# Down projection of a two-layer trunk: twelve instead of eight of 22 row tiles by seven products, the ordinary row tiles as lead

## The chip, the cores and the metric

The kernel runs on one core of a Trainium2 chip. A core has five engines that work side by side, each with an instruction queue of its own: TensorE (PE, matmuls and transposes), VectorE (DVE), ScalarE (ACT), GpSimd (POOL, here it issues accumulating DMAs) and SyncE (SP, here it issues loads and stores). SBUF is the working memory, PSUM holds matmul results in eight banks. The metric is device time in microseconds of one execution, the median of several runs.

## The reference

Two layers. Each layer is a half-step SwiGLU, a mixer (a gated linear recurrence and a windowed attention), and a second half-step SwiGLU, each with an RMS norm before and after it:

```python
def swiglu(h, w_gate, w_up, w_down):
    return (jax.nn.silu(h @ w_gate) * (h @ w_up)) @ w_down
...
for l in range(DEPTH):
    h = rms_norm(x, gn[0])
    x = x + 0.5 * rms_norm(swiglu(h, w_ffn1_gate[l], w_ffn1_up[l], w_ffn1_down[l]), gn[1])
    ...  # mixer
    h = rms_norm(x, gn[4])
    x = x + 0.5 * rms_norm(swiglu(h, w_ffn2_gate[l], w_ffn2_up[l], w_ffn2_down[l]), gn[5])
```

There are 512 tokens, 1024 model columns and 2816 inner columns, all in float32. The part in question is the product with `w_down`: (512 x 2816) @ (2816 x 1024), four times in the program. The 2816 inner columns are 22 row tiles of 128.

## The kernel before

**Float32 by three matmuls.** Every operand is split into a high part rounded to the fast format (`hi`, float32r) and the low rest (`lo`). A product is hi x hi + hi x lo + lo x hi, three matmuls (`mm3`). ScalarE makes the high part with a copy, VectorE the low part with a subtraction; `split_dma` makes the low part in another way, by a second ScalarE pass (the negated value) and an accumulating DMA that POOL issues.

**Weights.** `Stream` brings the weights in the order in which TensorE uses them. A raw unit of 128 x 1024 is loaded into `w32` (four buffers) by SP and rounded into `whi` and `wlo` (six buffers each, `WS`). An item is one rounded unit. Up to three items are made ahead (`AHEAD`), as long as fewer than six are in use. `Stream.quarter` makes the items of the seven products.

**The order of the work.** The order of TensorE's instructions is that of the program text; short side jobs (the recurrence, the attention, transposes) are put between by an estimate of the time (`Order`, `WAIT`). The instructions of the other engines are ordered at build time by a scheduler that works with its own estimates, except where `pin` keeps program order. On the chip each queue is then fixed. SBUF tiles of 128 x 512 come from one pool of 61 buffers (`big`), PSUM banks from two pools: five `acc` and three `aux`.

**The down projection (`down`, L636).** Its result is 512 x 1024: four token tiles `t` and two column halves `h`, eight accumulators `y[t][h]` of one bank each. `both(j, h)` adds two row tiles (2j and 2j+1) to one half: 4 x 2 x 3 = 24 matmuls of 128 x 512, with one weight item. Here the rows of the left operand, `src`, are split by `ready` shortly before they are used.

Eight of the 22 row tiles go by a scheme with seven instead of eight block products. The left operand is cut into two halves of tokens and two groups of row tiles, the weights into two groups of row tiles and two halves of columns; sums of these blocks are multiplied (products 1 to 7), and the results are added up. One product with four row tiles and two token tiles is 4 x 2 x 3 = 24 matmuls. `Late.sums` makes the sums of the left operand (`quarter_sums`: four VectorE operations of 128 x 256 per pair of row tiles) and splits them; `quarters` runs the products and adds the results with VectorE; products 2, 3 and 4 go straight into `y`.

So there is first a lead (row tiles 0 to 7, half 0, four calls of `both`), in which the operands of the products are made; then the products 1, 6, 2, 7, 5, 4, 3; then the last six row tiles of half 0; then the 14 ordinary row tiles of half 1. During the last four units of half 1 the results leave PSUM: `half` adds the products' sums and multiplies by the gains, `post` and `norm` add to x and normalize, `turn` transposes for the next stage. The rows of x and the gains come by `fetch`, ahead of half 1.

**The mixer.** `recurrence_scores` computes score blocks in steps. Between the steps it yields, and other matmuls run. The step after `WAIT["chunks"]` (1270 in the estimate's nanoseconds) is four matmuls of 128 x 256 on operands that VectorE scales at L1047 and L1048, with a copy by ScalarE at L1057.

Of the kernel before, what the change touches and what calls it, by code (L numbers as in the profile page):

```python
# [15 lines left out]
P = 128  # L16
D = 1024
S = 512
# [15 lines left out]
    head=2600.0, level=5000.0, last=3400.0, chunks=1270.0, blocks=350.0, norm=2370.0, gate=8000.0,  # L34
# [4 lines left out]
LEAD = 8  # L39
ORDER = ("p1", "p6", "p2", "p7", "p5", "p4", "p3")  # L40
DMAS = ()
# [4 lines left out]
def trunk(ctx: ExitStack, tc: tile.TileContext, xin, wall, gains, lbT, hgain, sinks, c_dist, c_mask, c_ident, out):  # L46
# [109 lines left out]
    class Stream:  # L156
# [36 lines left out]
        def rows(self, kt, fast):  # L193

            u0 = self.wall

            def pieces(j, h):
                b = [(4 * h + i) * kt + 2 * j for i in range(4)]  # L200
                return [(slice(i * 2 * P, (i + 1) * 2 * P), wall[u0 + n // 8][:, n % 8 * P : (n % 8 + 2) * P]) for i, n in enumerate(b)]

            def unit(j, h):
                c = 2 * j * P
                self.src[self.n] = [(None, wall[u0 + 4 * h : u0 + 4 * h + 4, :, c : c + 2 * P].rearrange("u p c -> p u c"))] if kt == 8 else pieces(j, h)
                self.plain(1)

            j0, later = LEAD // 2 if fast else 0, []
            if fast:
                for j in range(j0):  # L210
                    unit(j, 0)

                u = self.n
                for q in range(2):
                    self.src[u + q] = pieces(j0 + q, 0)
                    self.src[u + 2 + q] = pieces(j0 + 2 + q, 0)
                self.side[u + 1] = [pieces(j0 + q, 1) for q in range(4)]
                for k in ORDER:
                    for q in range(2):
                        it = Item(k, u + q + (2 if k in ("p2", "p4") else 0), 4)  # L220
                        it.base, it.q = u, q
                        self.items.append(it)
                self.t2 = [None, None]
                self.n += 4
                for j in range(j0):
                    later.append(j)
                j0 += 4
            for j in range(j0, kt // 2):
                unit(j, 0)
                later.append(j)  # L230
            for j in later:
                unit(j, 1)
            self.wall = u0 + kt

        def load(self, upto):
            while self.dma < min(upto, self.n):
                w = sb.tile([P, D], F32, tag="w32", name=nm("w32"), bufs=W32)
                u = self.dma
                if isinstance(self.src[u], list):
                    for c, a in self.src[u]:  # L240
                        nc.sync.dma_start(w.rearrange("p (m c) -> p m c", m=4) if c is None else w[:, c], a)
                else:
                    for c in (slice(0, D // 2), slice(D // 2, D)) if u == 0 else (slice(0, D),):
                        nc.sync.dma_start(w[:, c], wall[self.src[u]][:, c])
                self.raw[u] = w
                self.dma += 1
                if u in self.side:
                    self.b12, self.b22 = [], []
                    for i, ps in enumerate(self.side[u]):
                        v = [big(), big()]  # L250
                        for c, a in ps:
                            nc.sync.dma_start(v[c.start // S][:, c.start % S : c.start % S + 2 * P], a)
                        (self.b22 if i > 1 else self.b12).append(v)

        def quarter(self, it):

            self.load(it.base + 4)
            q, h = it.q, (slice(0, S), slice(S, D))
            if it.kind in ("p1", "p2", "p5", "p4"):
                w = [self.raw[it.u][:, c] for c in h]  # L260
            elif it.kind == "p6":

                t = sb.tile([P, D], F32, tag="tt", name=nm("tt"), bufs=2)
                self.t2[q] = w = [t[:, c] for c in h]
                for c in range(2):
                    t1 = self.raw[it.u][:, h[c]]
                    pin(nc.vector.tensor_tensor(t1, t1, self.b12[q][c], op=ALU.subtract))
                    pin(nc.vector.tensor_tensor(w[c], t1, self.b22[q][c], op=ALU.subtract))  # L268
            elif it.kind == "p3":
                w = self.b22[q]  # L270
            elif it.kind == "p7":

                w = self.b12[q]
                for c in range(2):
                    b21 = self.raw[it.base + 2 + q][:, h[c]]
                    pin(nc.vector.tensor_tensor(w[c], w[c], self.b22[q][c], op=ALU.add))
                    pin(nc.vector.tensor_tensor(b21, b21, self.t2[q][c], op=ALU.add))
            it.hi = sb.tile([P, D], F32R, tag="whi", name=nm("whi"), bufs=WS)
            it.lo = sb.tile([P, D], F32R, tag="wlo", name=nm("wlo"), bufs=WS)
            for c in range(2):  # L280
                nc.scalar.copy(it.hi[:, h[c]], w[c])
                if it.kind in DMAS:
                    nc.scalar.mul(it.lo[:, h[c]], w[c], -1.0)
                    nc.gpsimd.dma_start(it.lo[:, h[c]].bitcast(F32), w[c], accum_op=ALU.add)
                else:
                    nc.vector.tensor_tensor(it.lo[:, h[c]], w[c], it.hi[:, h[c]].bitcast(F32), op=ALU.subtract)  # L286
            self.done += 1
            self.flight += 1
            if it.kind in ("p5", "p4"):
# [181 lines left out]
    class Quarters:  # L471
# [4 lines left out]
        def operand(self, n):  # L476
# [4 lines left out]
            return [[v[:, i, :] for v in x[k]] for k in range(4)]  # L481
# [127 lines left out]
    class Late(Quarters):  # L609


        def __init__(self, src, k0):
            self.src, self.k0 = src, k0
            self.x1, self.x56, self.x37, self.t = [], [], [], []


        def sums(self):
            k = self.k0 + len(self.x56)
            a = [self.src[i][:, c] for i in (k, k + 4) for c in HALF]
# [3 lines left out]
            self.x56.append(pair_split(s))  # L623
            self.t.append(t)
            self.src[k] = ()

        def more(self, n):

            for i in range(len(self.x37), n):
                self.src[self.k0 + 4 + i] = split(self.src[self.k0 + 4 + i])  # L630
                self.x37.append(pair_split(self.t[i], split_dma))

        def raw(self, half, i):
            return [cut(self.src[self.k0 + 4 + k], HALF[half]) for k in range(4)] if i else self.x1

    def down(src, kt, l, n, nxt, fast):  # L636
# [8 lines left out]
        pre = Pre(*nxt) if nxt else None  # L645

        def ready(n):

            for i in range(min(n, kt)):
# [6 lines left out]
        def piece(b, t, h, j, i):  # L656
            st = cut(src[2 * j + i], slice(t * P, (t + 1) * P))
            mm3(y[t][h], st, [halves(w, i) for w in b[2:]], 2 * j + i == 0 and not (fast and h and t < 2), 2 * j + i == kt - 1)
# [20 lines left out]
        js = list(range(kt // 2))  # L679
        if fast:  # L680
            late = Late(src, LEAD)
            for j in range(LEAD // 2):
                ready(2 * j + EARLY)
                while len(late.x56) < min(4, 8 * (j + 1) / LEAD):
                    late.sums()
                both(j, 0)
            more = quarters(late, y)
            del js[LEAD // 2 : LEAD // 2 + 4]
        for j in js[LEAD // 2 if fast else 0 :]:
            ready(2 * j + 2 + EARLY)  # L690
            both(j, 0)
        if not fast:
            for t in range(TT):
                y[t][1] = aux() if t > 1 else acc()
        fetch()
        last = js[-TAIL:]
        for j in js[:-TAIL]:
            both(j, 1)

        warm = small([P, 1], "warm", 2)  # L700
        pin(nc.scalar.activation(out=warm, in_=src[last[0]][0][:, :1].bitcast(F32), func=AF.Sqrt, bias=eps_t, scale=0.0))
# [69 lines left out]
    def quarters(late, y):  # L771
# [3 lines left out]
        def product(n, o, start, stop=True):  # L775
            its = [ws.whole(), ws.whole()]
            for k in range(4):
                for t in range(2):
                    st = cut(late.operand(n)[k], slice(t * P, (t + 1) * P))
                    it = its[k // 2]  # L780
                    mv = [w.rearrange("p (m two c) -> p m two c", two=2, c=P)[:, :, k % 2, :] for w in (it.hi, it.lo)]
                    mm3(o[t], st, mv, start and k == 0, stop and k == 3)
# [12 lines left out]
        late.more(2)  # L795
        p = product(1, two(acc), True)
        p1, u2, u3, c12, c22 = (two(big) for _ in range(5))
        for t in range(2):
            nc.scalar.copy(p1[t], p[t])
        late.more(4)  # L800

        add(u2, product(6, two(aux), True), p1)
        product(2, [y[t][0] for t in (0, 1)], False, False)

        add(u3, product(7, two(acc), True), u2)
        p = product(5, two(aux), True)
        add(c12, p, u2)
        add(c22, p, u3)
        product(4, [y[t][0] for t in (2, 3)], False, False)
        for t in range(TT):  # L810
            y[t][1] = aux() if t > 1 else acc()
        product(3, [y[t][1] for t in (0, 1)], True, False)
# [638 lines left out]
```

## Time and profile before

| | |
|---|---|
| median of 3 runs | 2108.14 us (2106.92 to 2108.67) |
| the profiled execution's own time | 2106.95 us |
| its span, first to last instruction | 2104.9 us |
| TensorE busy | 2093.2 us |
| VectorE busy | 1549.3 us |
| ScalarE busy | 1122.6 us |
| granted TensorE clock, mean | 0.999 |
| the four down projections begin at | 241.1, 937.4, 1282.6, 1978.6 us |

In a group's line `L115 PE MATMUL acc<-whi,s 128*128 128x512 f32 x1264 | 414.0, 393 | 0.0` the first number behind the bar is the busy time of the group in microseconds, the second the mean of one in nanoseconds, the last the idle time of the engine just before them, with what ended it. Matmuls overlap each other, so their mean duration is longer than the distance between two. In the windows, each row is a stretch: its length, then busy time and count of PE, the weight loads, DVE, ACT and POOL, the granted clock, the DMA engines' busy share, and GB/s. `w<-wall` and `s<-wall` are loads of weights, `s<-s` at L400 and L401 the two halves of a split (cast and subtraction), L281 and L286 those of the seven products' weights, L324 and L331 those of the others. L458 to L462 are the sums in `quarter_sums`.

### The profile page before, as it was taken

To read this page: it belongs to the slowest core of one execution; us is meant where nothing else is said; L and a number is where in the kernel's file an instruction comes from. 1 tells how busy PE (TensorE), PEld (TensorE's weight loads), DVE (VectorE), ACT (ScalarE), POOL (GpSimd) and SP (SyncE) were. 2 spreads that over 40 slices of the span, in tenths; PEclk is the share of its full clock that TensorE was granted. 3 is DMA by queue.
4 is the path that set the end of the run, shared out by engine and by line. 5 is a ranking of instruction groups with operands and counts; after the bars stand their busy time and mean duration, and the time that the engine had idled before them with its cause. 6 is when DMAs were issued, how large, how long until landed. Compare 5 with 4: busy or idle time off the path is not lost.

```text
span 2104.9 us, 35214 instructions
## 1 busy us (share of the span) xinstructions
PE 2093.2 (99%) x13549; PEld 1875.4 (89%) x13549; DVE 1549.3 (74%) x2705; ACT 1122.6 (53%) x1899; POOL 154.2 (7%) x188
## 2 busy tenths in 40 slices
PE   9999999999999999999999999999999999999998
PEld 7899988877888999998899998898778989999987
DVE  5877886766776777789587778767686758777884
ACT  6555554446454555556355556444654545555562
POOL 0011000000000011110001110000000000111000
PEclk9999999999999999999999999999999999999999
DMA  8677653312236357774447775632122563677651
GB/s 247 152 181 184 176 164 127 111 61 70 72 101 201 127 123 181 181 194 128 151 114 176 183 181 149 190 121 91 51 81 61 136 190 106 158 182 181 182 164 47
DMA packets 148071, 298.35 MB, mean 142 GB/s; under 512 B 16992, under 2 KB 74816, under 8 KB 147904
## 3 DMA queue, kind: packets, MB, share of 16 engines
q1 hardware_dynamic: 122416, 228.16, 33.1%
q0 software_dynamic: 25344, 67.91, 18.7%
q8 instruction: 106, 1.74, 0.3%
q14 instruction: 61, 0.50, 0.1%
q10 hardware_dynamic: 144, 0.05, 0.0%
HBM read 213.43 MB, written 14.73 MB: 108 GB/s over the span
## 4 chain that ended last, share of the span: by engine, by line
PE 80%; DVE 9%; ACT 6%; issue 2%; DMA 2%; SPq 0%; ACTq 0%; DVEq 0%
PE acc L115 59%; PE aux L115 19%; ACT whi L324 2%; DMA w<-wall 2%; DVE s L401 1%; PE aux L125 1%; DVE wlo L331 1%; DVE wlo L286 1%; ACT s L400 1%; ACT m L894 1%; ACT wlo L328 1%; PE acc L125 1%; DVE tt L318 1%; DVE tt L311 1%; DVE tt L268 0%
## 5 line engine op out<-in xcount | busy, mean ns | idle before, releaser
L115 PE MATMUL acc<-s,whi 128*128 128x256 f32 (+1 forms) x4952 | 1059.4, 311 | 0.9 <-ACT whi L324 0.7
L115 PEld LDWEIGHTS acc<-s,whi 128*128 128x128 f32 x4952 | 808.0, 191 | 51.8 <-issue 3.2
L115 PE MATMUL acc<-s,wlo 128*128 128x256 f32 (+1 forms) x2476 | 766.6, 310 | 0.1
L115 PEld LDWEIGHTS acc<-s,wlo 128*128 128x128 f32 x2476 | 472.6, 191 | 25.2 <-DVE wlo L331 0.4
L324 ACT CAST whi<-w 128x1024 fp32r<-128x1024 f32 (+1 forms) x341 | 317.0, 948 | 259.2 <-PE acc L115 99.9
L115 PE MATMUL acc<-whi,s 128*128 128x512 f32 x1264 | 414.0, 393 | 0.0
L324 ACT CAST whi<-tt 128x1024 fp32r<-128x1024 f32 x154 | 161.4, 1048 | 326.6 <-DVE tt L318 182.8
L331 DVE TENSOR_TENSOR wlo<-w,whi 128x1024 fp32r<-128x1024 f32 (+1 forms) x181 | 218.1, 1215 | 156.5 <-ACT whi L324 149.4
L115 PEld LDWEIGHTS acc<-whi,s 128*128 128x128 f32 x1264 | 237.1, 188 | 54.9 <-ACT whi L324 1.6
L331 DVE TENSOR_TENSOR wlo<-tt,whi 128x1024 fp32r<-128x1024 f32 x154 | 188.0, 1221 | 97.4 <-ACT whi L324 97.3
L115 PE MATMUL acc<-wlo,s 128*128 128x512 f32 x632 | 246.9, 391 | 1.0 <-DVE wlo L286 1.0
L115 PE MATMUL aux<-s,whi 128*128 128x256 f32 (+1 forms) x1248 | 230.5, 285 | 0.0
L329 POOL DMA_DIRECT2D wlo<-w x160 | 137.8, 863 | 1259.6 <-ACT wlo L328 732.2
L115 PE MATMUL aux<-whi,s 128*128 128x512 f32 x592 | 196.8, 390 | 0.0
L115 PEld LDWEIGHTS aux<-s,whi 128*128 128x128 f32 x1248 | 195.2, 192 | 1.1 <-issue 0.5
L115 PE MATMUL aux<-s,wlo 128*128 128x256 f32 (+1 forms) x624 | 177.6, 285 | 0.0
L115 PEld LDWEIGHTS acc<-wlo,s 128*128 128x128 f32 x632 | 118.7, 188 | 25.6 <-DVE wlo L286 2.4
L115 PEld LDWEIGHTS aux<-whi,s 128*128 128x128 f32 x592 | 111.1, 188 | 22.9
L328 ACT ACTIVATE wlo<-w 128x1024 fp32r<-128x1024 f32 (+1 forms) x160 | 129.8, 844 | 0.0
L400 ACT CAST s<-s 128x512 fp32r<-128x512 f32 (+1 forms) x164 | 88.6, 580 | 70.7 <-DVE s L459 66.6
L115 PEld LDWEIGHTS aux<-s,wlo 128*128 128x128 f32 x624 | 119.8, 192 | 0.4
L115 PE MATMUL aux<-wlo,s 128*128 128x512 f32 x296 | 115.2, 389 | 0.0
(186 smaller groups left out, 2127.6 us busy)
## 6 DMA issues: line engine op xcount, KB each, us to landing
w<-wall SPq DMA_DIRECT2D x267, 512.0 KB, 3.7
wlo<-w POOLq DMA_DIRECT2D x83, 512.0 KB, 5.5
w<-wall SPq DMA_DIRECT2D x288, 128.0 KB, 3.2
wlo<-w POOLq DMA_DIRECT2D x77, 256.0 KB, 3.3
x_d<-s SPq DMA_DIRECT2D x48, 256.0 KB, 2.1
s<-x_d SPq DMA_DIRECT2D x48, 256.0 KB, 5.3
w<-wall SPq DMA_DIRECT2D x34, 256.0 KB, 3.0
s<-wall SPq DMA_DIRECT2D x64, 128.0 KB, 3.6
```

The costliest lines, as they stand in the source:

```text
L115: nc.tensor.matmul(o, lhsT, rhs, start=start, stop=stop)
L125: nc.tensor.transpose(o, src, ident)
L286: nc.vector.tensor_tensor(it.lo[:, h[c]], w[c], it.hi[:, h[c]].bitcast(F32), op=ALU.subtract)
L311: pin(nc.vector.tensor_tensor(self.t13[:, h[0]], w[:, h[0]], v[:, h[0]], op=ALU.add))
L318: pin(nc.vector.tensor_tensor(t[:, h[1]], t[:, h[0]], w[:, h[1]], op=ALU.add))
L324: i = nc.scalar.copy(it.hi[:, c], w[:, c])
L328: nc.scalar.mul(it.lo[:, c], w[:, c], -1.0)
L329: nc.gpsimd.dma_start(it.lo[:, c].bitcast(F32), w[:, c], accum_op=ALU.add)
L331: nc.vector.tensor_tensor(it.lo[:, c], w[:, c], it.hi[:, c].bitcast(F32), op=ALU.subtract)
L400: nc.scalar.copy(hi, src)
L401: nc.vector.tensor_tensor(lo, src, hi.bitcast(F32), op=ALU.subtract)
L894: nc.scalar.activation(out=m[:, 0:2, :], in_=m[:, 0:2, :], func=AF.Silu)
```

## The change

**Twelve row tiles.** `LEAD = 8` gives way to `SEVEN = 12`: row tiles 0 to 11 go by the seven products, with six row tiles each (36 matmuls), and three weight items instead of two. The ten last ones (12 to 21) are ordinary, and half 0 of all ten is the lead (five calls of `both`). Half 1 of the ten follows the products: one unit, and then the last four, in which the results leave.

**Order of the products.** 1, 3, 7, 2, 6, 4, 5. The raw side blocks (b22, b12) are six of two 128 x 512 buffers, formerly four. Sums of weights are made product by product: b12 + b22 for product 7, the block t2 from it, b22 + t2 after product 6, b21 + t2 for product 4. t2 has a buffer from `tt` or, the third, `m`. The subtraction for `wlo` is pinned to program order.

**Rounding product by product.** `late.sums` now splits a[0] (product 1) and the sums t (products 3 and 7, the low part by DMA); the sums s (products 5 and 6) and the second group of row tiles (products 2 and 4) are split only behind product 7, by `more` and `rest`, all with the low part by DMA. In the lead, a split row tile is dropped after its unit (`part`) and split again for half 1, apart from those that are already kept.

**PSUM.** `y[0][1]` and `y[1][1]` are `aux` and come behind product 1, `y[2][1]` and `y[3][1]` are `acc`, behind product 5. `fetch` now stands ahead of product 5. In the mixer, `chunks` is 2600.

```diff
-    head=2600.0, level=5000.0, last=3400.0, chunks=1270.0, blocks=350.0, norm=2370.0, gate=8000.0,
+    head=2600.0, level=5000.0, last=3400.0, chunks=2600.0, blocks=350.0, norm=2370.0, gate=8000.0,
...
-LEAD = 8
-ORDER = ("p1", "p6", "p2", "p7", "p5", "p4", "p3")
-DMAS = ()
+SEVEN = 12
+ORDER = ("p1", "p3", "p7", "p2", "p6", "p4", "p5")
...
+            lead = range(SEVEN // 2 if fast else 0, kt // 2)
+            for j in lead:
+                unit(j, 0)
             if fast:
...
+                u, n = self.n, SEVEN // 4
+                for q in range(n):
+                    self.src[u + q] = pieces(q, 0)
+                    self.src[u + n + q] = pieces(n + q, 0)
+                self.side[u + n - 1] = [pieces(n + q, 1) for q in range(n)], [pieces(q, 1) for q in range(n)]
...
-            for j in later:
+            for j in lead:
                 unit(j, 1)
...
         def quarter(self, it):
...
+            n, q, h = SEVEN // 4, it.q, (slice(0, S), slice(S, D))
+            self.load(it.base + n if it.kind == "p3" else it.u + 1)
+
+            def sums(o, x, y, op):
                 for c in range(2):
...
+                    pin(nc.vector.tensor_tensor(o[c], x[c], y[c], op=op))
+
+            raw = [self.raw[it.u][:, c] for c in h] if it.kind in ("p1", "p7", "p2", "p4") else None
+            if it.kind in ("p1", "p2"):
+                w = raw
+            elif it.kind in ("p3", "p5"):
                 w = self.b22[q]
             elif it.kind == "p7":
                 w = self.b12[q]
...
+                sums(w, w, self.b22[q], ALU.add)
+            elif it.kind == "p6":
+                w = self.t2[q]
+            else:
+                w = raw
+                sums(w, w, self.t2[q], ALU.add)
...
+                pin(nc.vector.tensor_tensor(it.lo[:, h[c]], w[c], it.hi[:, h[c]].bitcast(F32), op=ALU.subtract))
+            if it.kind == "p7":
+
+                t = sb.tile([P, D], F32, tag="m" if q == 2 else "tt", name=nm("t2"), bufs=1 if q == 2 else 2)
+                self.t2.append([t[:, c] for c in h])
+                sums(self.t2[q], raw, w, ALU.subtract)
+            elif it.kind == "p6":
+                sums(self.b22[q], self.b22[q], w, ALU.add)
...
     class Late(Quarters):
...
         def sums(self):
-            k = self.k0 + len(self.x56)
-            a = [self.src[i][:, c] for i in (k, k + 4) for c in HALF]
+            k = len(self.x1)
+            a = [self.src[i][:, c] for i in (k, k + self.n) for c in HALF]
             x = big(F32R, [P, 2, S // 2])
             self.x1.append(split(a[0], to=(x[:, 0, :], x[:, 1, :])))
             s, t = quarter_sums(a[0], a[2], a[1], a[3], True)
-            self.x56.append(pair_split(s))
-            self.t.append(t)
+            self.s.append(s)
+            self.x37.append(pair_split(t, split_dma))
             self.src[k] = ()
...
+        def rest(self):
+            for k in range(self.n, 2 * self.n):
+                self.src[k] = split_dma(self.src[k])
+
+        def more(self):
+            self.x37 = None
+            while self.s:
+                self.x56.append(pair_split(self.s.pop(0), split_dma))
...
         if fast:
...
+            late = Late(src)
+            for i, j in enumerate(js):
+                while len(late.x1) < min(late.n, (late.n * (i + 1) + 3) // 4):
                     late.sums()
+                for k in range(2 * j, min(2 * j + EARLY, kt)):
+                    if k not in part and not isinstance(src[k], tuple):
+                        part[k] = split(src[k])
                 both(j, 0)
...
+                for k in (2 * j, 2 * j + 1):
+                    part.pop(k, None)
+            more = quarters(late, y, fetch)
...
         p = product(1, two(acc), True)
+        late.x1 = None
+        p1, u3, c12, c22 = (two(big) for _ in range(4))
         for t in range(2):
             nc.scalar.copy(p1[t], p[t])
...
+        for t in range(2):
+            y[t][1] = aux()
+        product(3, [y[t][1] for t in (0, 1)], True, False)
+        p = product(7, two(acc), True)
+        late.rest()
+        late.more()
+        add(u3, p, p1)
+        product(2, [y[t][0] for t in (0, 1)], False)
+        p = product(6, two(acc), True)
+        add(c12, p, p1)
+        add(u3, p, u3)
+        product(4, [y[t][0] for t in (2, 3)], False)
+        fetch()
+        p = product(5, two(acc), True)
         add(c22, p, u3)
...
+        add(c12, p, c12)
...
-                for i in range(EARLY):
+                for i in range(SEVEN, SEVEN + EARLY):
                     a[i] = split(a[i])
```

More of the change, by code (lines that the diff above doesn't have):

```diff
@@ L769, in down, with quarters @@
         return pre
-    def quarters(late, y):
+    def quarters(late, y, fetch):
         def product(n, o, start, stop=True):
-            its = [ws.whole(), ws.whole()]
-            for k in range(4):
+            x = late.operand(n)
+            for k in range(late.n):
+                if k % 2 == 0:
+                    it = ws.whole()
+                mv = [w.rearrange("p (m two c) -> p m two c", two=2, c=P)[:, :, k % 2, :] for w in (it.hi, it.lo)]
                 for t in range(2):
[L779 to L782, printed above, removed]
+                    mm3(o[t], cut(x[k], slice(t * P, (t + 1) * P)), mv, start and k == 0, stop and k == late.n - 1)
                     ws.used((it, 1))
@@ L793, in two @@
             return [f(), f()]
-        late.more(2)
         p = product(1, two(acc), True)
-        p1, u2, u3, c12, c22 = (two(big) for _ in range(5))
+        late.x1 = None
+        p1, u3, c12, c22 = (two(big) for _ in range(4))
         for t in range(2):
             nc.scalar.copy(p1[t], p[t])
[L800 to L807, printed above, removed]
+        for t in range(2):
[10 more added lines that the diff above has]
+        product(4, [y[t][0] for t in (2, 3)], False)
+        fetch()
+        p = product(5, two(acc), True)
         add(c22, p, u3)
[L809 to L812, printed above, removed]
+        add(c12, p, c12)
         return [[(p1, u3)[t // 2][t % 2], (c12, c22)[t // 2][t % 2]] for t in range(TT)]
```

106 lines of the change are left out of this document (34 added, 72 removed).

## The prediction

> **What bounds the kernel now.** I read the page first, then the first down projection stretch by stretch, then TensorE's waits, and last the queues of ScalarE and VectorE at that projection's start.
>
> ```profile
> span 2104.9 us, 35214 instructions
> PE 2093.2 (99%) x13549; PEld 1875.4 (89%) x13549; DVE 1549.3 (74%) x2705; ACT 1122.6 (53%) x1899; POOL 154.2 (7%) x188
> PEclk9999999999999999999999999999999999999999
> ```
>
> TensorE is busy throughout at full clock, so the time moves with its matmuls and its waits. A matmul's price is read from unbroken runs of the chain that ended last (start, us, what, count):
>
> ```profile
> 334.59 10.88 PE acc L115 x48
> ...
> 354.02 4.09 PE aux L115 x18
> 358.12 8.67 PE acc L115 x72
> ```
>
> A 128x512 matmul costs 10.88 / 48 = 0.2267 us, a 128x256 one 8.67 / 72 = 0.120. Now the first down projection in four stretches (lead, seven products, rest of the first half, second half):
>
> ```profile
> 241.10:262.90 21.80, 21.80 (x98) 17.93 (x97) 20.17 (x40) 9.32 (x19) 0.00 (x0) 1.00 0.57 168
> 262.90:301.00 38.10, 37.81 (x166) 30.82 (x165) 36.22 (x58) 25.97 (x45) 3.44 (x4) 1.00 0.47 120
> 301.00:317.30 16.30, 16.30 (x74) 13.49 (x73) 8.86 (x11) 5.79 (x8) 0.00 (x0) 1.00 0.92 289
> 317.30:358.00 40.70, 40.70 (x190) 33.93 (x189) 22.50 (x41) 18.79 (x42) 0.61 (x2) 1.00 0.32 112
> ```
>
> The third busy time is VectorE's: 93% and 95% in the first 60 us, and yet TensorE is idle for 0.29 us only. The operands come just in time, so the order in which ScalarE and VectorE make them decides. TensorE's waits:
>
> ```profile
> PE acc L115 <- DVE wlo L286: 1.0, 4, 0.3
> PE aux L115 <- DVE s L1048: 0.9, 2, 0.5
> PE aux L115 <- ACT s L1057: 0.7, 2, 0.3
> ```
>
> **Matmuls: -10.9 us.** Before, a down projection has 14 ordinary row tiles of 24 matmuls and seven products of 24: 504. After, 10 x 24 + 7 x 36 = 492. Twelve fewer, four times, make 48 x 0.2267 = 10.9, in full, since TensorE is the bound.
>
> **Old waits: -2.6 us.** The waits for L286 (1.0, one per down projection) belong to the old sums, which are gone; product 7's, late next if any, stand twelve 512-wide VectorE operations (7.2 us) behind the lead's last, and 96 matmuls (21.8 us) pass meanwhile. The longer "chunks" puts each mixer's four score matmuls behind 21 others of 0.2267 (4.8 us), past the L1048 scaling and L1057 copy that they waited for: -0.9 - 0.7. If the next step is then late, this is 0.
>
> **More work beside TensorE: 0.** Its prices, and those of the next part:
>
> ```profile
> 248.11 0.39 ACT L400 CAST s<-s 128x256 fp32r<-128x256 f32 x1
> ...
> 269.62 2.18 ACT L281 CAST whi<-w 128x512 fp32r<-128x512 f32 x4
> ```
> ```profile
> 283.91 4.89 DVE L286 TENSOR_TENSOR wlo<-w,whi 128x512 fp32r<-128x512 f32 x8
> ```
> ```profile
> L324 ACT CAST whi<-w 128x1024 fp32r<-128x1024 f32 x262 | 274.1, 1049 | 259.2 <-PE acc L115 99.9 <-PE aux L115 99.1 <-DMA w<-wall 37.1
> L331 DVE TENSOR_TENSOR wlo<-w,whi 128x1024 fp32r<-128x1024 f32 x179 | 216.8, 1221 | 156.5 <-ACT whi L324 149.4 <-DMA s<-x_d 4.2 <-DMA w<-wall 2.3
> L281 ACT CAST whi<-w 128x512 fp32r<-128x512 f32 x64 | 35.9, 617 | 3.4 <-DMA w<-wall 3.3
> L400 ACT CAST s<-s 128x256 fp32r<-128x256 f32 x28 | 10.7, 398 | 0.1
> L401 DVE TENSOR_TENSOR s<-s,s 128x512 fp32r<-128x512 f32 x136 | 89.2, 686 | 14.0 <-ACT s L400 13.7
> L401 DVE TENSOR_TENSOR s<-s,s 128x256 fp32r<-128x256 f32 x28 | 11.2, 418 | 0.0
> ```
>
> A 512-wide ScalarE cast takes 0.62 and follows the last one at (2.18 - 0.62) / 3 = 0.52; a 512-wide VectorE operation follows at 0.60 (4.89 / 8, its end taken off). Per down projection VectorE gets 18 operations of 512 and 10 of 256 and loses four of 1024: 18 x 0.60 + 10 x 0.34 - 4 x 1.22 = +9.3. ScalarE gets 36 of 512 and two of 256 and loses four of 1024: 36 x 0.52 + 2 x 0.4 - 4 x 1.05 = +15.3. The windows leave VectorE 29 us free and ScalarE 57. The cover is 112 us of matmuls; without it VectorE's 9.3 x 4 would be paid. POOL issues 14 more accumulating DMAs each time:
>
> ```profile
> q0 software_dynamic: 25344, 67.91, 18.7%
> ```
>
> Twelve of them, of 0.25 MB, serve products 2 and 6. By this row (0.187 x 2104.9 us for 67.91 MB) they take 17 us of all DMA engines; they are issued from product 3 on, 72 matmuls (16 us) before product 2 begins and 108 (24 us) before product 6, and are read one row tile at a time: hidden. On SP the rows of x and the gains (`fetch`) move ahead of the second half's weights. They wait for buffers that product 7 and those DMAs free, 144 matmuls (32 us) before the second half: 0.
>
> **The lead's operands: +60.4 us, which decides.** The rounded weights (`whi`, `wlo`) go round a ring of six. Before, four lead items and two of product 1 fill it. Now there are five lead items, so product 1's second and third item need the places of the first two, free only when those lead units are through. ScalarE's queue in the built program, in its order (lines of the changed kernel):
>
> ```
> L274 TensorCopy whi_540_3042<-w32_481_2793 128x512 x2
> L274 TensorCopy whi_551_3094<-w32_484_2816 128x512 x2
> L396 TensorCopy s_502_2887<-s_80_440 128x256
> L406 TensorCopy s_505_2896<-s_504_2891 128x512
> L407 Activation s_506_2897<-s_504_2891 128x512
> ...
> L396 TensorCopy s_520_2962<-s_377_2173 128x512
> L396 TensorCopy s_522_2966<-s_397_2300 128x512
> ```
>
> (L274 rounds a weight, L396, L406 and L407 come from `late.sums`; the dots are the same three twice more.) whi_551 waits for the last matmul of the lead's second unit, at 2 x 24 x 0.2267 = 10.9 us. Behind it stand three `late.sums`, and behind these s_520, the row tile that the third unit needs at the same 10.9 us. VectorE's next operation reads s_502, so it stops too. What the turns between the two cost is in the chain, where before does the same sums:
>
> ```profile
> 248.93 0.33 DVE s L401
> 249.26 0.34 DVE s L458
> 249.60 0.34 DVE s L462
> 249.93 0.35 DVE s L459
> 250.28 0.02 issue
> 250.30 0.02 ACTq L400
> 250.32 0.04 issue
> 250.36 0.63 ACT s L400
> 250.99 0.02 issue
> 251.01 2.23 DVE s L401 x4
> ```
>
> VectorE's 256-wide operations follow at 0.34, the last 0.42; a hand-over costs 0.08 to ScalarE, 0.02 back. From the second unit's end:
> - ScalarE: whi_551 2 x 0.52, s_502 0.39: 1.43
> - VectorE: five of 256: 4 x 0.34 + 0.42 = 1.78
> - twice: ScalarE two of 512 and one of 256, 2 x 0.52 + 0.40 = 1.44; VectorE the three that hang on it, 2 x 0.34 + 0.42 = 1.10 (two others fit meanwhile): 5.08
> - ScalarE, two more and s_520: 2 x 0.52 + 0.62 = 1.66
> - six hand-overs 0.30, and 0.15 from and to TensorE (estimate, from these)
>
> Sum 10.4. Then the third unit runs 5.44, while the fourth unit's s_536 takes four VectorE operations of 512 and five of 256 (4 x 0.60 + 1.78), 1.44, 1.10, 1.66 and hand-overs 0.20: 8.6. That is 2.9 more, after 0.25 for the third unit's own low part (0.02 + 0.68 behind its cast, wanted after 2 x 0.2267). The last two units wait in the same way 0.7 and 0.9 (low parts of 0.25 each, two casts of 0.5, a VectorE lag of 0.3). Together 15.1 per down projection, 60.4 for four. Bounds: if VectorE were done beforehand, the twelve casts alone, 8 x 0.52 + 0.62 + 3 x 0.34 = 5.8; with every operation at its full mean (0.617, 0.398, 0.686, 0.418) instead of its spacing, 17.7. I take the sum, since its rows are the same operations in the same alternation.
>
> The Trainium skill ("TensorE: Matmul & The Clock Gate", Architectural detail) says that ScalarE and VectorE are strict first-in first-out, which is what this term needs; with an engine that passed s_520 ahead the sum would be the first rival's.
>
> **The end of three down projections: +0.9 us.** In the next stage the third accumulator takes the bank of the second turn, the fourth that of the last output tile:
>
> ```profile
> 357.99 0.86 DVE L590 SCALAR_TENSOR_TENSOR s<-acc,g_sb,s 128x256 fp32r<-128x256 f32 x2
> 358.78 0.68 DVE L711 TENSOR_TENSOR s<-aux,s 128x512 f32<-128x512 f32 x1
> ```
>
> The next stage starts at 358.12; its third block is due 6 x 0.12 = 0.72 later, the bank is free at 358.85; the fourth at 359.2, free at 359.46. That is 0.3 each, between 0 and 0.9 (one 512-wide operation later).
>
> Sum against the profiled execution's own 2106.95: + 60.4 + 0.9 - 10.9 - 2.6 = +47.8, 2154.8. The median of the runs is 1.2 above it: 2156.
>
> **Rivals.**
> 1. Faster: the third unit's operands aren't held. For it speaks that before nothing waits there (21.80 of 21.80). It decides where s_520 stands in ScalarE's queue: ahead of whi_551 and of the sums' casts it is made in time. Then 2106.95 + 0.9 - 10.9 - 2.6 = 2094.3, median 2095. The built order speaks against it. Chance 0.05.
> 2. VectorE has the sums ready, only the casts stand between: 4 x 5.8 = 23.2 in place of 60.4, 2119. Against it: VectorE's queue has the low part of s_502 ahead of the sums. 0.11.
> 3. The clock falls in the 10 us hole. The trace shows it after the last wait:
>
> ```profile
> PE acc L125 <- DVE s L730: 2.9, 1, 2.9
> ```
> ```profile
> 2090.00:2096.00 6.00, 6.00 (x33) 4.99 (x31) 3.66 (x6) 1.60 (x4) 0.00 (x0) 1.00 0.26 82
> 2100.20:2104.90 4.70, 0.68 (x4) 0.28 (x2) 0.38 (x1) 0.58 (x1) 0.00 (x0) 0.50 0.37 112
> ```
>
> The granted clock (third number from the end) is 0.50 there. Half a clock for the third unit adds at most 5.44, of which the 2.9 that it waits for afterwards hides a part: 0 to 2.5 each, 2156 to 2166; if the fourth is slow too, up to 2172. The same page's Part 1 has the clock halve after an idle window of about 3.4 us and return after about 3.4 busy ones; by that alone 1.7 us are lost and hidden, the sum stays 2156. The end of the trace agrees with the halving. 0.14 for 2160 and more.
>
> **How the numbers follow.** The forecast has 0.69, own range 2148 to 2164 (12% on 60.4), so 2156. The range, 2142 to 2172, takes in the third rival and part-way cases towards the second. A change of 0.2% is about what the measurement can tell. Slower: 0.69 + 0.14 + 0.11, faster 0.05, same 0.01 left between.
>
> **What would show it.** TensorE's waits should name the lead's casts, one of 10 us at the third unit in each down projection and one of 1 to 3 us at the fourth; ScalarE idle until the second unit's end; the stretch from the first product on as dense as before; 48 matmuls fewer. Wrong would be no hole in the lead (rival 1), a hole of 6 us (rival 2), or holes in the products, which I price at nothing.

## The result and the profile after

The changed kernel takes 2156.95 us (median, 2155.76 to 2157.71), the kernel before beside it 2108.2: a ratio of 1.023, 95% interval 1.0216 to 1.0245. It is 48.8 us slower; the forecast was 2156. The profiled execution took 2157.71, with a span of 2155.9.

The page of the changed kernel, the same rows as before:

```profile
span 2155.9 us, 35610 instructions
PE 2098.2 (97%) x13501; PEld 1870.9 (87%) x13501; DVE 1593.0 (74%) x2801; ACT 1185.3 (55%) x2035; POOL 202.5 (9%) x244
```

There are 48 TensorE instructions fewer, as counted, but TensorE is busy for 97% of a longer span instead of 99%. Its waits (engine and tile, line, what it waited for: us in total, times, longest):

```profile
PE acc L114 <- ACT s L396: 46.9, 9, 10.7
PE acc L124 <- DVE s L739: 2.9, 1, 2.9
PE acc L114 <- DVE s L586: 1.1, 3, 0.4
```

46.9 us go to the cast of a row tile (L396), in nine waits with a longest of 10.7; the rows of old sums (L286) and of the mixer (L1048, L1057) are gone. The first down projection as one window, of the kernel before and of the changed one (length, then busy time and count of PE, PEld, DVE, ACT, POOL, the granted clock, DMA share, GB/s):

```profile
241.10:358.00 116.90, 116.61 (x523) 96.17 (x522) 87.76 (x148) 59.87 (x112) 4.05 (x6) 1.00 0.50 150
```
```profile
241.65:372.60 130.95, 118.88 (x510) 95.94 (x509) 98.41 (x171) 75.84 (x147) 16.09 (x20) 0.95 0.62 163
```

It is 14.1 us longer; by the starts of the matmuls the other three are 12.5, 12.8 and 12.7 longer, 52.1 together. A loss by the starts is the time from one start to another less 0.2267 us for each matmul between them. It is larger than in the view of waits, which counts from the modelled end of the matmul before, and matmuls overlap. By this count the four leads lose 17.7, 16.1, 16.0 and 16.0 us, 65.8 in all, and no matmul of the products or of half 1 waits. The stretches of the lead show where (two units, the hole, the third unit, the fourth):

```profile
241.65:252.55 10.90, 10.90 (x50) 8.83 (x48) 5.88 (x8) 4.59 (x8) 0.00 (x0) 1.00 0.88 247
252.55:263.20 10.65, 0.17 (x1) 0.00 (x0) 5.56 (x15) 5.86 (x12) 1.81 (x3) 0.71 0.96 256
263.20:269.00 5.80, 5.63 (x17) 4.45 (x18) 4.93 (x11) 2.27 (x6) 0.77 (x1) 0.64 0.61 130
269.00:274.30 5.30, 4.08 (x15) 2.37 (x14) 2.98 (x6) 3.66 (x8) 1.73 (x2) 0.99 0.49 85
```

After two dense units TensorE does one matmul in 10.65 us. VectorE and ScalarE are each busy for little more than half of that time: they take turns. The third unit then runs at a granted clock of 0.64, 17 matmuls in 5.63 us where 0.2267 each would give 25. The queues of ScalarE and VectorE at that place (start, us, engine, line, what; in brackets the idle time before and what ended it):

```profile
247.21 0.63 ACT L906 ACTIVATE m<-m 128x512 f32<-128x512 f32 x1 [0.97 <-DVE m L894]
247.75 1.12 ACT L274 CAST whi<-w 128x512 fp32r<-128x512 f32 x2
252.76 1.14 ACT L274 CAST whi<-w 128x512 fp32r<-128x512 f32 x2 [3.89 <-PE aux L114]
253.80 0.40 ACT L396 CAST s<-s 128x256 fp32r<-128x256 f32 x1
```
```profile
247.87 0.69 DVE L907 SCALAR_TENSOR_TENSOR s<-m 128x512 f32<-128x512 f32 x1 [0.76 <-ACT m L906]
254.23 0.42 DVE L397 TENSOR_TENSOR s<-s,s 128x256 fp32r<-128x256 f32 x1 [5.67 <-ACT s L396]
```

This is the order that the prediction read: the last gate (L906), product 1's second weight, then its third, for which ScalarE stands idle for 3.89 us, because its buffer in the ring of six is still in use by the lead's second unit. All of `late.sums` stands behind it, and VectorE is idle for 5.67 us.

### The profile page after: what moved, and what is told of

Read it like the earlier page. It is cut to its first block, busy times and chain, and to the rows that moved or that the text cites. A ratio compares the mean times of both kernels' runs of the same rounds, so it can differ in the third digit from the quotient of the medians.

```text
span 2155.9 us, 35610 instructions
## 1 busy us (share of the span) xinstructions
PE 2098.2 (97%) x13501; PEld 1870.9 (87%) x13501; DVE 1593.0 (74%) x2801; ACT 1185.3 (55%) x2035; POOL 202.5 (9%) x244
## 5 line engine op out<-in xcount | busy, mean ns | idle before, releaser
L114 PE MATMUL acc<-whi,s 128*128 128x512 f32 x1344 | 449.0, 402 | 47.3 <-ACT s L396 46.9
L320 ACT CAST whi<-w 128x512 fp32r<-128x512 f32 (+1 forms) x325 | 300.2, 943 | 190.8 <-PE acc L114 123.5
L114 PEld LDWEIGHTS acc<-whi,s 128*128 128x128 f32 x1344 | 256.1, 191 | 117.9 <-ACT s L396 53.1
L320 ACT CAST whi<-tt 128x1024 fp32r<-128x1024 f32 x154 | 161.4, 1048 | 327.1 <-DVE tt L314 188.4
L327 DVE TENSOR_TENSOR wlo<-w,whi 128x1024 fp32r<-128x1024 f32 (+1 forms) x165 | 199.4, 1214 | 103.4 <-ACT whi L320 102.4
L114 PE MATMUL acc<-wlo,s 128*128 128x512 f32 x672 | 265.9, 396 | 0.0
L327 DVE TENSOR_TENSOR wlo<-tt,whi 128x1024 fp32r<-128x1024 f32 x154 | 188.1, 1221 | 99.1 <-ACT whi L320 98.9
L114 PE MATMUL aux<-whi,s 128*128 128x512 f32 x480 | 159.2, 390 | 0.0
L114 PEld LDWEIGHTS acc<-wlo,s 128*128 128x128 f32 x672 | 128.7, 192 | 24.9
L397 DVE TENSOR_TENSOR s<-s,s 128x512 fp32r<-128x512 f32 (+1 forms) x148 | 88.6, 622 | 66.4 <-ACT s L396 66.3
L114 PEld LDWEIGHTS aux<-whi,s 128*128 128x128 f32 x480 | 90.1, 188 | 18.7
L396 ACT CAST s<-s 128x512 fp32r<-128x512 f32 (+1 forms) x148 | 77.9, 562 | 48.3 <-DVE s L455 43.6
```

The costliest lines, as they stand in the source:

```text
L114: nc.tensor.matmul(o, lhsT, rhs, start=start, stop=stop)
L320: i = nc.scalar.copy(it.hi[:, c], w[:, c])
L327: nc.vector.tensor_tensor(it.lo[:, c], w[:, c], it.hi[:, c].bitcast(F32), op=ALU.subtract)
L396: nc.scalar.copy(hi, src)
L397: nc.vector.tensor_tensor(lo, src, hi.bitcast(F32), op=ALU.subtract)
```

## The experiments

Lines shift by up to 12 from kernel to kernel: L396, L398 and L397, L401 are the two halves of a split, L274 and L275 or L277 those of the products' weights, L320, L322 and L327, L329 those of the other weights.

### splits_first: the row tiles ahead of the sums

```diff
-                while len(late.x1) < min(late.n, (late.n * (i + 1) + 3) // 4):
-                    late.sums()
-                for k in range(2 * j, min(2 * j + EARLY, kt)):
+                for k in range(2 * j, min(2 * j + EARLY + 2, kt)):
                     if k not in part and not isinstance(src[k], tuple):
-                        part[k] = split(src[k])
+                        part[k] = split(src[k], hold=True)
+                while len(late.x1) < min(late.n, (late.n * (i + 1) + 3) // 4):
+                    late.sums()
```

(`hold` pins the cast; the casts of product 1's weights are pinned too.)

> The edit: in the lead the row tiles of the next units (two more of them, up to six ahead) are split before late.sums instead of behind it, and ScalarE keeps program order for these casts and for the casts of product 1's weights. No operation is added or taken away. Theory (the order of ScalarE's queue holds the third unit's operand): the waits in the lead go. In the changed kernel a down projection became 14.1, 12.5, 12.8 and 12.4 us longer, 51.8 in all, although its matmuls fell by 10.9 and an old wait of 1.0 went, and the end took 1.5: so the lead costs 62.2. Without it 2157 - 62 = 2095 us (2092 to 2100), ratio to the kernel before 0.994, and no wait for a cast of the lead above 1 us. Rival A (too much work in the lead, in whatever order: VectorE and ScalarE have the sums and the splits of twelve row tiles to do in 27 us): the waits only move to later units or to product 1, and the time stays at 2150 to 2160. Rival B (the twelve row tiles bring other waits, in products 3 to 5, which the hole hides now): 2105 to 2130, with waits after the lead.

Measured: 2107.79 us (2105.03 to 2110.71), ratio to the kernel before 0.9998 (0.9989 to 1.0008). The lead is dense, 27.20 us busy of 27.20, first row below, so that the order of the queues made the holes and Rival A falls for the lead. But the time is 13 us above 2095. The new waits:

```profile
240.80:268.00 27.20, 27.20 (x123) 22.54 (x122) 19.89 (x41) 13.34 (x26) 3.45 (x4) 1.00 0.82 223
```
```profile
PE aux L114 <- DVE s L401: 5.8, 11, 0.8
PE acc L114 <- ACT whi L274: 2.3, 3, 1.0
PE acc L114 <- DVE wlo L277: 1.2, 4, 0.3
```

The first is in half 1, the other two at product 1's third weight. By the starts of the matmuls half 1 loses 3.2, 2.8, 3.5 and 0.4 us in the four down projections and product 1 loses 1.9, 1.3, 0.6 and 1.7, 15.4 together. So Rival B has the time (2105 to 2130), though not the place: the products behind the first lose only 0.1. In the changed kernel, and in weights_later with 8.6 to 9.2 us lost in each lead, nothing waits behind the lead; so the stall had hidden the work that the change adds.

### weights_later: half of the remedy

```diff
-                nc.scalar.copy(it.hi[:, h[c]], w[c])
+                i = nc.scalar.copy(it.hi[:, h[c]], w[c])
+                if it.kind == "p1":
+                    pin(i)
```

(The casts of the lead's row tiles and of `late.sums`' a[0] are pinned as well; the program text is not moved.)

> The edit: nothing is moved in the program, but ScalarE keeps program order among late.sums' first cast, the lead's casts and the casts of product 1's weights, so that these weights no longer stand ahead of the sums. It does half of the other edit. Theory: the chain of sums and casts (10.4 us worked out, less 1.04 for the cast that goes behind it, less 0.15) need no longer wait for the second unit's end; it can begin when ScalarE is through with the last gate, at 247.84 in the trace of the changed kernel, 6.2 us after the lead's start. Then s_520 is there at about 257, and the third unit, due at 252.5, waits 3 to 5.6 us instead of 10.8; the fourth waits up to 2.9 (no half clock hides it), the rest as now. Per down projection some 8 to 10 us are left of 15.5, the time is 2095 + 32 to 40 = 2127 to 2135 (2120 to 2140). Rival (the sums' place alone makes the hole, the wait for the ring of six adds nothing): 2150 to 2160. Other rival (the ring alone makes it): 2095.

Measured: 2128.94 us (2126.97 to 2129.91), ratio 1.0098 (1.0083 to 1.0113), in the expected 2127 to 2135.

```profile
PE acc L114 <- ACT s L398: 21.3, 8, 4.6
```

The third unit waits 4.1 to 4.8 us instead of 10.8. With splits_first, this divides the hole: some 6.4 us come from the weights of product 1, above all the one that waits for its place in the ring, the rest from the sums that stand ahead of the row tile. The fourth unit waits 0.9 to 1.6 instead of the 2.9 that the expectation allowed; the clock again falls behind the first wait. From the third unit's first matmul to the fourth's it is 8.80 us, as in the changed kernel.

### early6: two row tiles ahead, by one number

```diff
-W32, WS, AHEAD, TAIL, PLAIN, FIRST, EARLY, LATE = 4, 6, 3, 4, 4, 7, 4, 8
+W32, WS, AHEAD, TAIL, PLAIN, FIRST, EARLY, LATE = 4, 6, 3, 4, 4, 7, 6, 8
```

> The edit: EARLY from 4 to 6, one number: the row tiles 16 and 17 of the third unit are split during the gates, and in the lead each unit's row tiles are asked for one unit earlier; the weights' casts and the sums stay where they are. Theory: the third unit no longer waits; the same chain now ends in front of the fourth unit's row tile, which is due 5.4 us later: 10.8 - 5.4 = 5.4 us of wait there, then up to 2.9 at the fifth, then about 1: some 9 per down projection, 2095 + 37 = 2132 us (2122 to 2138). Rival A (too much work in the lead): 2150 to 2160, since the last unit ends no earlier. Rival C (the wait is for the third unit's weight or a load, not for its row tile): the wait stays at the third unit with 10 us, 2157.

Measured: 2138.7 us in one run, 0.7 above the expected range.

```profile
PE acc L114 <- ACT s L396: 25.8, 8, 5.6
PE acc L114 <- DVE s L586: 4.0, 3, 1.3
PE acc L124 <- DVE s L750: 0.7, 2, 0.6
```

The third unit no longer waits; the fourth waits 5.7 us in all four down projections. Rival C is out, the queue theory had 5.4. By the starts the leads lose 11.6, 9.9, 11.4 and 9.9 us, more than the 9 expected; in the first and the third the clock falls a second time, and the fifth unit takes 7.8 and 7.7 us instead of 6.2. The rest of the surplus is at the other end: L586, the turn of the next stage, holds TensorE for 4.0 instead of 1.1 us, and L750 0.7. Why two more kept row tiles delay the turn stays open.

### dummies: what the half clock costs

```diff
         def both(j, h, dummy=None):
             b = ws.next(8, TT)
+            if dummy:
+                for _ in range(44):
+                    nc.tensor.matmul(dummy, b[2][:, :P], halves(b[2], 0), start=True, stop=True)
```

> The edit: 44 matmuls of 128x512 with no use are put ahead of the lead's third unit, into a bank that product 1 overwrites; 44 x 0.2267 = 10.0 us of the hole of 10.8. It asks what the half clock behind the hole costs. Theory (hidden): with the clock at 1.0 the third unit runs in 5.4 us instead of about 8, but the fourth unit's operand comes no earlier, so that its wait grows from 1.2 to 2.9 and more: time as the changed kernel's, 2153 to 2159; the granted clock 1.0 in the lead, the wait at the third unit about 0.9. Rival (the half clock costs in full: about 10 us at half speed, some 2.7 to 5 us in each of four down projections): 2137 to 2146, and no longer wait at the fourth unit.

Measured: 2159.48 us (2158.74 to 2161.21), ratio to the kernel before 1.0245 (1.023 to 1.0261): 0.5 above the expected range, the time of the changed kernel within 2.5 us, and far from the rival's 2137 to 2146. The hole filled, the third unit and the fourth, in the first down projection:

```profile
252.40:263.20 10.80, 10.10 (x44) 7.77 (x42) 6.27 (x17) 6.21 (x14) 2.59 (x3) 1.00 0.94 252
263.20:269.00 5.80, 5.32 (x23) 4.05 (x22) 4.93 (x12) 1.99 (x5) 0.72 (x1) 1.00 0.35 69
269.00:275.00 6.00, 3.68 (x10) 2.65 (x11) 4.20 (x10) 3.10 (x7) 1.01 (x2) 0.80 0.51 87
```

The third unit has 23 matmuls in the time in which it had 17. Nothing is gained: the fourth unit then waits 2.95 to 2.97 us, 11.8 in the four, where the changed kernel waits 0.95 to 1.51. What the clock took there was time that TensorE would have waited: from the third unit's first matmul to the fourth's it is 8.80 us in both kernels, first the changed one, then this one:

```profile
263.37 0.80 PE L114 MATMUL acc<-whi,s 128*128 128x512 f32 x1 [10.65 <-ACT s L396]
272.17 0.50 PE L114 MATMUL acc<-whi,s 128*128 128x512 f32 x1 [1.22 <-ACT s L396]
```
```profile
262.52 0.50 PE L114 MATMUL acc<-whi,s 128*128 128x512 f32 x1 [0.70 <-ACT s L396]
271.32 0.50 PE L114 MATMUL acc<-whi,s 128*128 128x512 f32 x1 [2.80 <-ACT s L396]
```

The run was not wholly at full clock: behind this longer wait it fell in three of the four down projections (0.80 in the last row), which fits the few us above.

### rows_later and third_weight: the two waits that are left

```diff
             grow.append(g)
+            if not fast:
+                rows()
+
+        def rows():
             for t in range(TT):
...
             both(j, 1)
+        if fast:
+            rows()
```

> The edit: on top of splits_first, SP loads the eight tiles of x's rows behind the weights of half 1 instead of ahead of the last two of them (the gains stay where they are). In splits_first the lead's holes are gone, but TensorE waits in the first units of half 1 for low parts of row tiles; counted from the starts of its matmuls these waits are 2.7, 2.8 and 2.7 us in three down projections. ScalarE there had waited 5.5 us for a weight from memory, VectorE's low part of this weight came behind it, and behind that the four additions of product 5 and the row tiles. Theory (the rows of x delay the weights, the chain through VectorE does the rest): these waits go, 2107.8 - 8 = 2100 us (2098 to 2103). Rival (VectorE is simply late with its work of the products, whatever the weights do): 2106 to 2110.

In splits_first, SP loads six of the eight tiles of x's rows ahead of the fifth and last weight of half 1 (four pieces, issued at 323.08; the second to fourth are the twelve at 310.78, L236 is the next stage):

```profile
310.78 7.51 SPq L233 DMA_DIRECT2D w<-wall  x12
318.40 3.63 SPq L678 DMA_DIRECT2D s<-x_d  x6
323.08 1.76 SPq L233 DMA_DIRECT2D w<-wall  x4
324.95 0.85 SPq L678 DMA_DIRECT2D s<-x_d  x2
325.89 5.40 SPq L236 DMA_DIRECT2D w<-wall  x4
```

Its ScalarE can cast this weight only at 328.62, and in VectorE's queue the low part of it stands ahead of product 5's additions (L802) and the row tiles (L401):

```profile
328.62 1.05 ACT L322 CAST whi<-w 128x1024 fp32r<-128x1024 f32 x1 [5.46 <-DMA w<-wall]
```
```profile
329.71 1.23 DVE L329 TENSOR_TENSOR wlo<-w,whi 128x1024 fp32r<-128x1024 f32 x1 [2.05 <-ACT whi L322]
330.85 2.48 DVE L802 TENSOR_TENSOR s<-acc,s 128x512 f32<-128x512 f32 x4
333.73 0.69 DVE L401 TENSOR_TENSOR s<-s,s 128x512 fp32r<-128x512 f32 x1 [0.40 <-ACT s L398]
```

With the rows behind the weights the same cast starts 2.12 us earlier, of which 0.6 are gained ahead of half 1 (rows_later):

```profile
326.50 1.05 ACT L322 CAST whi<-w 128x1024 fp32r<-128x1024 f32 x1 [3.96 <-DMA w<-wall]
```

Measured: 2101.28 us (2098.52 to 2103.61), ratio 0.9967 (0.9955 to 0.9979), 6.5 us less than splits_first, as expected. Its waits for L401 are down to 3.2, not to nothing.

third_weight makes four weights ahead during the lead:

```diff
             late = Late(src)
+            ws.most = AHEAD + 1
...
+            ws.most = AHEAD
             more = quarters(late, y, fetch)
```

> The edit: on top of rows_later, the number of weights made ahead is four instead of three during the lead, so that the cast of product 1's third weight stands before the last of late.sums in ScalarE's queue. In splits_first TensorE waited for it 1.0 us and for its low part, 1.2 to 1.8 us together, in each of the four down projections. Theory: these 5.0 us go as well: 2100 - 5 = 2095 us (2093 to 2099), which is the time that the first rival of the prediction had for the change without a hole, ratio to before 0.994. Rival (ScalarE and VectorE have no time left, the wait moves to product 1's operand or to product 3): as rows_later, 2098 to 2103.

Measured: 2098.11 us (2097.36 to 2099.47), ratio 0.9953 (0.9941 to 0.9966): 10 us faster than the kernel before, 59 faster than the changed one. It beats both. Its waits:

```profile
PE aux L114 <- DVE s L401: 3.1, 3, 1.5
PE acc L114 <- DVE s L590: 1.5, 3, 0.5
```

The rows of L274 and L277 are gone. The gain is 3.2 us instead of 5, and the time lies in the ranges of both the theory and the rival. By the starts both have a part: product 1 no longer loses anything (5.2 us in rows_later), and products 3 to 5 lose 1.9 us that they did not before, in pieces too short for the view of waits.

### two_more_split: a miss

```diff
-            ready(2 * j + 2 + EARLY)
+            ready(2 * j + 4 + EARLY)
             both(j, 1)
```

> The edit: on top of third_weight, two more row tiles are split ahead of half 1's first unit (four instead of two), so that in ScalarE's and VectorE's queues they stand ahead of a weight of the next stage. third_weight still waits once in the first three down projections for such a row tile's low part, 0.95, 1.63 and 1.02 us by the starts of the matmuls; there two 1024-wide low parts (2.35 us) stand ahead of it on VectorE. Theory: these 3.6 us go, 2098 - 3.5 = 2094.5 us (2093 to 2097), ratio 0.9935. Rival (VectorE is full there, another operand is late next, a weight of the next stage for instance): 2097 to 2099.

Measured: 2099.28 us (2098.11 to 2099.86), ratio 0.9958 (0.9945 to 0.9972): no gain over third_weight, as the rival had it (0.3 above its range). L401 still costs 2.8 us, now in four waits:

```profile
PE aux L114 <- DVE s L401: 2.8, 4, 0.8
PE acc L114 <- DVE s L590: 1.7, 3, 0.6
```

VectorE's queue there, in the first down projection:

```profile
328.32 1.23 DVE L329 TENSOR_TENSOR wlo<-w,whi 128x1024 fp32r<-128x1024 f32 x1 [1.27 <-ACT whi L322]
329.46 2.48 DVE L810 TENSOR_TENSOR s<-acc,s 128x512 f32<-128x512 f32 x4
331.86 0.68 DVE L401 TENSOR_TENSOR s<-s,s 128x512 fp32r<-128x512 f32 x1
...
335.99 0.68 DVE L401 TENSOR_TENSOR s<-s,s 128x512 fp32r<-128x512 f32 x1
336.60 1.22 DVE L329 TENSOR_TENSOR wlo<-w,whi 128x1024 fp32r<-128x1024 f32 x1
337.73 1.28 DVE L401 TENSOR_TENSOR s<-s,s 128x512 fp32r<-128x512 f32 x2
```

From 328.32 on it has no gap (no brackets); another order only changes which operand is late.

### chunks_back: the mixer's step alone

```diff
-    head=2600.0, level=5000.0, last=3400.0, chunks=2600.0, blocks=350.0, norm=2370.0, gate=8000.0,
+    head=2600.0, level=5000.0, last=3400.0, chunks=1270.0, blocks=350.0, norm=2370.0, gate=8000.0,
```

> The edit: the changed kernel with chunks at 1270 again, nothing else. Theory: the waits for the scaling and for the copy ahead of the mixer's four score matmuls come back, 0.9 and 0.7 us, and nothing else differs: 2157 + 1.6 = 2158.6. Rival (the longer chunks did nothing, the waits went for another reason): no such rows among TensorE's waits, 2157.

Measured: 2159.06 us in one run. The two waits are back, at the size that they had before (the lines are 12 higher):

```profile
PE aux L114 <- DVE s L1060: 0.9, 2, 0.5
PE aux L114 <- ACT s L1069: 0.7, 2, 0.3
```

One run cannot resolve 1.6 us; the rows do. The second wait is not one of the score matmuls, though: its copy reads their result, and the 64x256 matmuls of another step wait for it.

## Why the prediction was right, and where it was not

**Matmuls, -10.9.** The count is right (13549 to 13501). That they count in full agrees with third_weight: its span is 9.1 us below that of before (2104.9 to 2095.8), and -10.9 - 2.6 + 3.1 + 1.5 (its two waits above) = -8.9.

**Old waits, -2.6.** Right in both parts: no wait for the sums of product weights is left in the changed kernel, and chunks_back returns 0.9 and 0.7. By the starts they were larger, 2.7 and 2.4 us. And the reading of the copy (L1057) was wrong: the score matmuls did not wait for it, the 64x256 matmuls behind them did, and in the changed kernel such matmuls stand ahead of the score matmuls.

**The lead's operands, +60.4.** The mechanism was right, and the size came within 9%: 65.8 us by the starts. Worked out and measured, in each down projection: the hole 10.4 and 10.8; from the third unit's first matmul to the fourth's 8.6 and 8.80; the fourth unit 6.1 and 6.51, in the first down projection 7.79; the fifth 6.3 and 6.25 to 6.58. The hole's two causes are shown separately by weights_later and splits_first. Of the 8.80, the wait of the fourth unit is only 1.38, 1.07, 0.95 and 1.51 instead of 2.9, since the third unit ran some 2 us longer at half clock. That is the third rival's mechanism, which did occur, and which cost next to nothing there, as dummies shows; only in the first down projection a second slow stretch made the fourth unit 1.3 us longer. The bounds of this term do not fit each other: 5.8 is for the hole alone, 17.7 for all of the 15.1. The 62.2 in splits_first's expectation is too small: it takes off the 1.5 at the end, which lies behind the stretches compared, and counts the old waits as 1.0.

**End of three down projections, +0.9.** Too small: 0.53, 0.53 and 0.52, 1.6 together, for the turn (L586). It is all at the third accumulator, where the working had 0.01; the 0.26 at the fourth did not come.

**More work beside TensorE, 0.** The number was right for this kernel, its reason was not. The sizes hold (first down projection: VectorE +10.7 against 9.3, ScalarE +16.0 against 15.3, 14 POOL instructions more). But the prediction named 112 us of matmuls as the cover, and for `fetch` the 144 matmuls ahead of half 1. In splits_first TensorE waits 15.4 us behind the lead with the same operations, in part as the rows of x delay the weights and VectorE gets behind (rows_later takes 5.6 of them away in half 1). The changed kernel loads seven of the eight tiles ahead of the same weight, and nothing waits; there this weight is issued 9.3 us ahead of half 1 in each down projection, in splits_first 4.3 to 5.3. So the cover was the hole: while TensorE stood for 16 us, the other queues could catch up.

**The sum, +47.8.** By the starts the parts are +65.8 less the 0.2 that the leads lost before, -10.9, -5.1 and +1.6, which makes +51.2; the spans differ by 51.0. The lead's surplus and the old waits partly cancel, and the medians differ by 2 us less than the profiled executions (48.8 against 50.8). That 2156 came within 1 us is partly luck; the mechanism and the size are not.

**The first rival, 2095.** For the same reason as that of the side work its price was 13 us too low. Without the hole the change gives 2107.8, no gain at all; 2098 takes two more edits. The second rival (casts only) is excluded by VectorE's 5.67 us of idle time ahead of the first low part.

## What to carry to other kernels

When a change adds items to a ring of buffers, look up in the built queues which instruction now waits for a place in it, and what stands behind it on its engine: here one such cast, with the sums behind it, cost six times what the saved matmuls bring. A price of nothing for added side work holds only together with the stall that gives it its time; after a remedy, count each queue again, that of the loads among them. And where one engine is nearly full, a better order of two operands moves a wait instead of removing it.

## What the runs showed of the hardware

In the changed kernel's first down projection the granted clock is half for 10.24 us from the middle of the hole on, and a second time for 3.42 us. In the fourth it falls once, and a similar wait at its fourth unit changes nothing:

```profile
257.12:267.36 10.24, 3.99 (x9) 3.11 (x10) 7.01 (x17) 4.46 (x10) 2.58 (x3) 0.50 0.92 223
270.77:274.18 3.41, 2.19 (x7) 1.03 (x7) 1.68 (x3) 3.22 (x7) 0.86 (x1) 1.00 0.64 112
274.18:277.60 3.42, 3.42 (x9) 2.64 (x9) 2.67 (x7) 0.63 (x2) 0.00 (x0) 0.50 0.18 33
2045.70:2049.12 3.42, 2.07 (x7) 0.78 (x5) 1.34 (x3) 3.38 (x7) 0.86 (x1) 1.00 0.61 106
2049.12:2052.53 3.41, 3.41 (x16) 2.74 (x16) 3.02 (x8) 0.43 (x2) 0.00 (x0) 1.00 0.28 47
```

In each of the ten traces the changes of the granted clock lie whole multiples of 3.413 us apart, so it is set once per window of a fixed grid. What decides is how much of one such window TensorE is idle, and not how long one wait is. The four down projections of the ten traces have 1363 windows at full clock. Counted by the starts of the matmuls, the 22 behind which the clock fell were idle for 2.04 to 3.41 us of their 3.41; none of the others was idle for more than 2.11. The border is thus near 2.05 us, 60% of a window, which is worked out from these traces alone; five windows lie between 2.04 and 2.11, three with a fall and two without.

This is why a short wait can do it. The wait of 1.38 us in the first down projection falls wholly into the window from 270.77 on, and smaller ones behind it bring that window to 2.04 us. The window of the fourth down projection that holds the wait of 1.51 us has 2.05, just at the border, and the clock stays. In dummies the clock fell behind three of four waits of 2.95 to 2.97 us, with 2.24 to 2.51 us in one window; the fourth wait was divided between two windows, 1.71 and 1.64 with the small waits, and the clock stayed. Back at full clock it came behind windows with at most 0.35 us idle; with 0.74 or more it stayed at half. The Trainium skill ("TensorE: Matmul & The Clock Gate", Part 1) has the clock fall after an idle window of about 3.4 us and return after as long a busy one, with windows that run freely. The traces agree on the window and on the return; for the fall it need not be idle throughout.
